# Value projection of the first layer in three column passes over four PSUM banks, with the gate columns in the first pass

## The chip, the cores and the metric

The kernel runs on one core of one Trainium2 chip. The metric is the device time of one launch in microseconds (us). The engines of the core work side by side: TensorE (PE, with its weight loads as PEld) does matmuls into PSUM, VectorE (DVE) and ScalarE (ACT) do elementwise work, GpSimd (POOL) does memsets here, and SyncE (SP) issues most of the loads and stores. PSUM has eight banks of 512 float32 columns in each of 128 partitions. This kernel hands them out as two `ps` tiles of one bank, two `pc` tiles of one bank and two `pm` tiles of two banks.

## The reference

The model has 1024 tokens of width 1024 and two layers: an mLSTM mixer with an MLP, then latent attention with an MLP. The change is in the mixer of the first layer. Of the reference, what it computes there:

```python
def mlstm_mixer(h, w_in, gate_b, head_g, w_out):
    proj = h @ w_in                      # (S, 3088)
    q, k, v, ig, fg, og = jnp.split(proj, splits, axis=-1)   # 512, 512, 1024, 8, 8, 1024
    ...
    i_pre = (ig + gate_b[0]).transpose(0, 2, 1)
    f_pre = (fg + gate_b[1]).transpose(0, 2, 1)
    hh = mlstm_chunkwise(heads(q, A_QK_DIM), heads(k, A_QK_DIM), heads(v, A_V_DIM), i_pre, f_pre)
    hh = rmsnorm(hh.transpose(0, 2, 1, 3), head_g).reshape(B_, S, A_V_W)
    return (hh * jax.nn.sigmoid(og)) @ w_out
```

There are eight heads. The values `v` are columns 1024 to 2047 of `w_in`, 128 for each head; the two gates are the 16 columns behind them, 2048 to 2063, one input gate and one forget gate for each head. `mlstm_chunkwise` goes over chunks of 128 tokens: inside a chunk it weighs scores of q and k by decays that come from the gates (running sums and running maxima along the tokens) and multiplies them with the values; between chunks it carries a state.

## The kernel before, in words

**Precision.** Every large product is made of three: an operand is split into a high part (`hi`, rounded to float32r) and the rest (`lo`), and `mm3` (L230 to L234) adds lo x hi, hi x lo and hi x hi in PSUM. So each matmul of a projection stands three times, on L232, L233 and L234.

**Weights.** `wload` (L204 to L224) loads a block of a weight matrix into one of four `raw` buffers of 128 x 1024 (L132), then `wsplit` casts it to its high part on ScalarE (L189) and subtracts that on VectorE to get the low part (L190). High and low parts take two of eight `ws` buffers, so four blocks can be ready ahead. `wload` runs at high priority. The `raw` buffers are taken in turn, in the order of the program, and they are shared with the background work below.

**Order.** The program is written out by generators that are woven into each other; then a scheduler orders the instructions of each engine by a simulated timeline, and may draw an instruction forward when its data and buffers are there. Buffers of a kind are always given out in the order of the program. `with_bg(g, bgs, n)` (L1880) runs n background steps for each step of g; `weave(main, fill, per)` (L71) and `weave_n` (L60) run `per` steps of a filling generator for each step of the main one; `weave` runs the rest of the filling one behind it, `weave_n` doesn't.

**Background.** `bgs` computes the modulation vectors of later stages. A chunk (`ada_chunk`, L348) loads four blocks of 512 KB into `raw` (L353), adds each, multiplied by the condition, into the one `tma` buffer on VectorE (L358 for the first row block, L360 for the other seven), makes two empty steps, and then turns the result with four transposes into a `pc` tile (`ada_turn`, L340) and reduces it on VectorE (L342, L343). That is seven steps, four of them with a load. The next chunk needs `tma` again.

**Halves.** The tokens are worked on in two halves of 512 (four tiles of 128). The normalised input of a half lies transposed, `h.hi[k]` and `h.lo[k]` for k of 0 to 7 (128 features x 512 tokens).

- `gates_in` (L626) of a half loads the 16 gate columns, spreads them over a zeroed 128 x 128 block for each k (the high parts at columns 0 to 7 and 32 to 39, the low parts at 64 to 71 and 96 to 103), and runs 16 matmuls of 512 columns into a `ps` tile (L642, L643): all of h goes through the array twice for 16 columns.
- `gates0` (L702) is a serial chain on VectorE and ScalarE over tiles of 8 x 512: the sums of the gates and biases (L707 to L711), log-sigmoid, running sums (L724), running maxima (L730), exponentials, the rows of `RM` (L744 to L751); then 12 small transposes (L756) and the copy of `gc` (L758).
- `qk_pairs` (half 0) and `qk_in` (L648, half 1) make queries and keys. In half 1 each of eight blocks is 24 matmuls of 512 columns into a `ps` tile, copied out on ScalarE (L198, L202).
- `v_in` (L657) makes the values with the tokens as rows: for each of four column blocks of 256 it loads two weight blocks (four k each); for each of four token tiles 24 matmuls of 256 columns go into one `ps` tile, which is copied to the value buffers on VectorE (L685) for odd tiles and on ScalarE (L687) for even ones. It makes 16 steps.
- `intra0` (L761) makes, for each of four pairs of heads, two decays (a matmul of a mask, L772, and one of `RM`, L775, into a `pc` tile, then four exponentials on ScalarE, L779, which need `gc`), eight score blocks into one `pm` tile (L787), their product on VectorE (L792), and a scaling of the queries (L795 to L797). It makes five steps for a pair.
- `chunks0` (L814) then goes over the chunks with `pm` tiles for the numerators (L831, L836); beside it run the output gates `og0` (L690, in `ps`) and, in half 0, the norm of the other half, `norm0`.

In half 0 `gates_in` comes first, with one background step for each of its three steps; then the activations of half 1 are loaded (`load_x1`), and then `v_in`, with one background step for each of its steps, runs woven with `intra0` at 1.5. In half 1 `gates_in` comes first too; then queries and keys (each step doubled by `twice`) and values form one main generator of 32 steps. Its first six steps run alone, with `split_o` of half 0 behind the fourth, and the rest runs with 1.7 background steps and 0.8 steps of `intra0` for each.

## Time and profile before

| | |
|---|---|
| median of 3 runs | 2370.01 us (2367.67 to 2371.02) |
| the profiled execution | 2373.3 us |
| its span, first to last instruction | 2371.2 us |
| granted TensorE clock | 0.996 |
| TensorE busy | 2334.8 us |
| VectorE, ScalarE busy | 1605.2 us, 1099.8 us |

A row of the timeline reads: start in us from the beginning of the span, duration in us, engine, line of the code, operation, output<-inputs, shape, number of merged instructions, and in brackets the idle time before it with what ended it. A row of the groups reads: line, engine, operation, names and shapes, count, then busy us, mean ns of one, and the idle us of the engine just before them. The shape of a matmul gives the stationary block and the moving one: 128x512 is 512 moving columns. Matmuls overlap, so a duration is longer than the distance from one start to the next. SPq is the queue of SyncE, where loads are issued.

### The profile page before, as it was taken

How to read it: one execution, taken by the hardware profiler on the slowest of the kernel's cores; microseconds unless marked ns; L12 is line 12 of the kernel's file. 1: busy time of each engine (PE TensorE's matmuls, PEld its weight loads, DVE VectorE, ACT ScalarE, POOL GpSimd, SP SyncE). 2: the span in 40 equal slices, each digit the busy share in tenths (PEclk: the TensorE clock that was granted, in tenths of full speed). 3: DMA queues.
4: the chain of work that ended last, by engine and by line, in shares of the span. 5: the costliest groups of instructions: out<-in, count | busy, mean ns of one | idle time of the engine just before them, and what ended most of it. 6: DMA issues, size and time to landing. Idle time of an engine off the chain costs nothing.

```text
span 2371.2 us, 32533 instructions
## 1 busy us (share of the span) xinstructions
PE 2334.8 (98%) x12197; PEld 1967.3 (83%) x12197; DVE 1605.2 (68%) x2657; ACT 1099.8 (46%) x1826; POOL 147.6 (6%) x345
## 2 busy tenths in 40 slices
PE   7999999999999999999999999999999999999998
PEld 5888888788888888888888888888888888989997
DVE  6667866868666677877774967766566478457556
ACT  4355334655333464434444544434434445655543
POOL 1000000000001210111110110001001000000000
PEclk9999999999999999999999999999999999999999
DMA  9453564544656966667754675885544552657552
GB/s 312 143 145 89 181 184 137 170 130 150 187 178 166 313 184 197 185 200 205 227 157 117 196 208 176 269 272 167 173 129 132 147 169 86 189 175 218 165 183 89
DMA packets 408350, 420.77 MB, mean 177 GB/s; under 512 B 27427, under 2 KB 310112, under 8 KB 404608
## 3 DMA queue, kind: packets, MB, share of 16 engines
q1 hardware_dynamic: 402272, 385.02, 51.9%
q0 software_dynamic: 5920, 33.66, 6.5%
q8 instruction: 96, 1.57, 0.3%
q14 instruction: 62, 0.51, 0.1%
HBM read 359.37 MB, written 92.80 MB: 191 GB/s over the span
## 4 chain that ended last, share of the span: by engine, by line
PE 90%; DVE 4%; DMA 3%; ACT 2%; issue 1%; SPq 0%; DVEq 0%; ACTq 0%
PE ps L232 16%; PE ps L233 15%; PE ps L234 15%; PE pm L232 10%; PE pm L233 10%; PE pm L234 10%; PE pc L234 2%; PE pc L232 2%; PE pc L233 2%; DMA raw<-in_mlp_w_dram 1%; PE pc L1637 1%; DMA raw<-in_a_w_in_dram 1%; DVE wl L190 1%; PE pm L836 1%; PE pm L1523 1%
## 5 line engine op out<-in xcount | busy, mean ns | idle before, releaser
L190 DVE TENSOR_TENSOR wl<-raw,wh 128x1024 fp32r<-128x1024 f32 (+2 forms) x382 | 458.5, 1203 | 385.8 <-ACT wh L189 281.4
L189 ACT CAST wh<-raw 128x1024 fp32r<-128x1024 f32 (+2 forms) x382 | 394.0, 1035 | 657.9 <-PE ps L232 241.8
L232 PE MATMUL ps<-k,wl 128*128 128x512 f32 (+1 forms) x1464 | 560.3, 383 | 2.6 <-ACT k L695 1.4
L234 PE MATMUL ps<-k,wh 128*128 128x512 f32 (+1 forms) x1464 | 551.6, 377 | 0.0
L233 PE MATMUL ps<-k,wh 128*128 128x512 f32 (+1 forms) x1464 | 550.7, 376 | 0.0
L232 PEld LDWEIGHTS ps<-k,wl 128*128 128x128 f32 x1464 | 275.7, 188 | 56.5 <-issue 3.6
L234 PEld LDWEIGHTS ps<-k,wh 128*128 128x128 f32 x1464 | 275.5, 188 | 51.7 <-issue 0.7
L233 PEld LDWEIGHTS ps<-k,wh 128*128 128x128 f32 x1464 | 275.9, 188 | 50.0 <-issue 1.9
L198 DVE TENSOR_TENSOR k<-k,pm 128x512 f32<-128x512 f32 (+1 forms) x254 | 211.2, 860 | 87.2 <-PE pm L234 86.1
L232 PE MATMUL pm<-hd,wl 128*128 128x512 f32 x512 | 201.1, 393 | 0.5 <-ACT hd L472 0.5
L233 PE MATMUL pm<-hd,wh 128*128 128x512 f32 x512 | 199.5, 390 | 0.2 <-DVE hd L473 0.2
L234 PE MATMUL pm<-hd,wh 128*128 128x512 f32 x512 | 199.4, 390 | 0.0
L232 PE MATMUL pm<-wh,hd 128*128 128x512 f32 x488 | 192.2, 394 | 3.9 <-ACT raw L1529 3.7
L233 PE MATMUL pm<-wl,hd 128*128 128x512 f32 x488 | 190.5, 390 | 0.0
L234 PE MATMUL pm<-wh,hd 128*128 128x512 f32 x488 | 190.3, 390 | 0.0
L360 DVE SCALAR_TENSOR_TENSOR tma<-raw,cond,tma 128x512 f32<-128x512 f32 x168 | 125.7, 748 | 20.0 <-DMA raw<-in_kv_ada_w_dram 13.8
L1529 ACT ACTIVATE raw<-pm,sm 128x128 f32<-128x128 f32 (+3 forms) x64 | 47.4, 741 | 155.1 <-DVE sm L1528 118.2
L473 DVE TENSOR_TENSOR hd<-tmp,hd 128x512 fp32r<-128x512 f32 x128 | 88.0, 689 | 40.4 <-ACT hd L472 39.8
L232 PEld LDWEIGHTS pm<-hd,wl 128*128 128x128 f32 x512 | 96.2, 188 | 20.9 <-ACT hd L472 0.9
L233 PEld LDWEIGHTS pm<-hd,wh 128*128 128x128 f32 x512 | 96.2, 188 | 20.5 <-DVE hd L473 0.5
L234 PEld LDWEIGHTS pm<-hd,wh 128*128 128x128 f32 x512 | 96.2, 188 | 20.2
L985 POOL COPY sm<-sm 128x1 f32<-128x1 f32 x128 | 51.9, 412 | 967.2 <-DVE sm L984 930.3
(385 smaller groups left out, 4064.1 us busy)
## 6 DMA issues: line engine op xcount, KB each, us to landing
raw<-in_mlp_w_dram SPq DMA_DIRECT2D x240, 512.0 KB, 4.3
raw<-in_ada_w_dram SPq DMA_DIRECT2D x80, 512.0 KB, 4.3
raw<-in_a_w_in_dram SPq DMA_DIRECT2D x48, 512.0 KB, 4.8
sums<-in_mlp_w_dram POOLq DMA_DIRECT2D x96, 256.0 KB, 4.8
raw<-sums SPq DMA_DIRECT2D x64, 256.0 KB, 3.7
xs<-k SPq DMA_DIRECT2D x40, 256.0 KB, 3.6
raw<-in_kv_ada_w_dram SPq DMA_DIRECT2D x16, 512.0 KB, 3.9
raw<-in_a_w_out_dram SPq DMA_DIRECT2D x16, 512.0 KB, 5.0
```

The lines of the kernel that those rows point to most:

```text
L189: nc.scalar.copy(hi[:, :n], r[:, :n])
L190: i = nc.vector.tensor_sub(lo[:, :n], r[:, :n], hi[:, :n].bitcast(F32))
L198: return f(*a, **k)
L232: nc.tensor.matmul(o, ll, rh, start=start, stop=False, **m)
L233: nc.tensor.matmul(o, lh, rl, start=False, stop=False, **m)
L234: pe_last[0] = nc.tensor.matmul(o, lh, rh, start=False, stop=stop, **m)
L360: nc.vector.scalar_tensor_tensor(acc, r[:, kk], cond[:, k : k + 1], acc, ALU.mult, ALU.add)
L473: nc.vector.tensor_sub(lo, u, hi.bitcast(F32))
L836: nc.tensor.matmul(nv[:, r, i], hf.PT[p_][:, r, cs], v[2 * p_ + r], start=g == 0, stop=True,)
L985: now = nc.gpsimd.tensor_copy(seen, flag)
L1523: nc.tensor.matmul(o[:, :w], qh, kh, start=False, stop=True)
L1529: nc.scalar.activation(pr[:, :n], f, AF.Exp, bias=m, scale=SCALE, accum_out=l)
```

## The change

Values and gates of a half are made together. `v_in` goes over three column passes. The first holds heads 6 and 7 and the 16 gate columns (256 + 16 = 272 columns, which lie side by side in `w_in`), the second heads 0 to 2 and the third heads 3 to 5 (384 columns each). A pass holds the sums of all four token tiles in both `pm` tiles, one bank for each token tile, and goes over k in groups: three k to a weight block in the first pass (three blocks), two in the others (four blocks each), so eleven weight blocks instead of eight. After every second token tile of a weight block there is a step: 22 steps. In the last k group of a pass the finished banks are copied out, the even tile on ScalarE and the odd one on VectorE.

The gate columns now come out with the tokens as rows. VectorE copies them into a zeroed `tmp` tile, and `gates_in` turns them with four transposes into a `pc` tile. They hold the full sum, so `gates0` drops its additions of a low part (two copies go, two fused operations become plain ones). The scores of `intra0` move from a `pm` tile to the two `ps` tiles.

The order changes with it. In half 0 the first pass (six steps) runs before `load_x1`, then the gate chain and `intra0` are woven into the other passes at 1.5; background steps run at 0.73 for each of the 22 steps. In half 1 the first pass runs before the queries and keys, with `split_o` before its last step; queries, keys and the other passes then run with 1.5 background steps for each, and the gates and `intra0` at 0.8.

The diff (in `v_in` cut to its core):

```diff
@@ gates_in
-        h = hf.h
-        wg = raw(F32R).rearrange("p (a b) -> p a b", b=P)
-        nc.gpsimd.memset(wg.bitcast(F32), 0.0)
...
-        gp = ps()
-        for k in range(KD):
-            nc.tensor.matmul(gp, wg[:, k], h.lo[k], start=k == 0, stop=False)
-            nc.tensor.matmul(gp, wg[:, k], h.hi[k], start=False, stop=k == KD - 1)
+        gp = pc()
+        for t in range(4):
+            nc.tensor.transpose(gp[0:64, ts(t, P)], hf.graw[:, t], ident)
         hf.gp = gp
@@ v_in
-        for j in range(4):
-            w0 = wload([(0, 0, wcols(w_in, 1024 + j * 256, 256, 0, 4))], 256)
-            w1 = wload([(0, 0, wcols(w_in, 1024 + j * 256, 256, 4, 4))], 256)
...
+        hf.graw = tmp()[:, :256].rearrange("p (t c) -> p t c", c=64)
+        nc.gpsimd.memset(hf.graw, 0.0)
+        for h0, nh, kg in ((6, 2, 3), (0, 3, 2), (3, 3, 2)):
+            n = nh * P + (16 if h0 == 6 else 0)
+            b = [pm(), pm()]
+            for k0 in range(0, KD, kg):
+                nk = min(kg, KD - k0)
+                w = wload([(0, 0, wcols(w_in, 1024 + h0 * P, n, k0, nk))], n)
+                for t in range(4):
+                    for k in range(nk):
+                        kk = k0 + k
+                        mm3(
+                            b[t // 2][:, t % 2, :n], h.hi[kk][:, ts(t, P)], h.lo[kk][:, ts(t, P)],
+                            w[0][:, k], w[1][:, k], kk == 0, kk == KD - 1,
+                        )
+                    if t % 2 and k0 + nk == KD:
+                        b2 = b[t // 2]
+                        if h0 == 6:
+                            nc.vector.tensor_copy(
+                                hf.graw.rearrange("p t (g c) -> p t g c", c=32)[:, t - 1 : t + 1, :, 0:8],
+                                b2[:, :, 256:272].rearrange("p t (g c) -> p t g c", c=8),
+                            )
+                        for e in range(2):
...
+                            copy = nc.vector.tensor_copy if e else nc.scalar.copy
...
                     if t % 2:
...
+                        yield
@@ gates0
-        nc.vector.tensor_copy(t1, gp[64:72])
-        nc.vector.scalar_tensor_tensor(t1, gp[0:8], col(GB, 1)[0:8], t1, ALU.add, ALU.add)
-        nc.vector.tensor_copy(t2, gp[96:104])
+        nc.vector.tensor_scalar(t1, gp[0:8], col(GB, 1)[0:8], None, ALU.add)
         nc.vector.tensor_copy(t3, gp[32:40])
-        nc.vector.scalar_tensor_tensor(t2, t3, col(GB + 1, 1)[0:8], t2, ALU.add, ALU.add)
+        nc.vector.tensor_scalar(t2, t3, col(GB + 1, 1)[0:8], None, ALU.add)
@@ intra0
-            st = pm()
+            st = [ps(), ps()]
...
-                        st[:, r, ts(j, P)], kp[ts(r, 64), ts(j, P)], qp[ts(r, 64), ts(j, P)],
+                        st[r][:, ts(j, P)], kp[ts(r, 64), ts(j, P)], qp[ts(r, 64), ts(j, P)],
...
-                nc.vector.tensor_mul(PT[:, r], st[:, r], E[r])
+                nc.vector.tensor_mul(PT[:, r], st[r], E[r])
@@ the order
-    drain(with_bg(gates_in(hfs[0]), bgs, 1))
+    main = with_bg(v_in(hfs[0]), bgs, 0.73)
+    for _ in range(6):
+        next(main)
     x1 = load_x1()
-    drain(weave(with_bg(v_in(hfs[0]), bgs, 1), intra0(hfs[0]), 1.5))
+    drain(weave(main, chain(gates_in(hfs[0]), intra0(hfs[0])), 1.5))
...
-    drain(gates_in(hfs[1]))
-    main = chain(twice(qk_in(hfs[1])), v_in(hfs[1]))
-    for _ in range(4):
-        next(main)
-    drain(split_o(hfs[0]))
-    for _ in range(2):
-        next(main)
-    drain(weave_n(with_bg(main, bgs, 1.7), intra0(hfs[1]), 0.8))
+    v1 = v_in(hfs[1])
+    for n in range(6):
+        next(v1)
+        if n == 4:
+            drain(split_o(hfs[0]))
+    main = chain(twice(qk_in(hfs[1])), v1)
+    drain(weave_n(with_bg(main, bgs, 1.5), chain(gates_in(hfs[1]), intra0(hfs[1])), 0.8))
```

More of the change, by code (lines that the diff above doesn't have):

```diff
@@ new lines, in v_in @@
+        nc.gpsimd.memset(hf.graw, 0.0)
[20 more added lines that the diff above has]
+                        for e in range(2):
+                            i = b2[:, e, : nh * P].rearrange("p (a b) -> p a b", b=P)
+                            v = hf.v[t - 1 + e]
+                            copy = nc.vector.tensor_copy if e else nc.scalar.copy
+                            if h0 == 6:
+                                for o in range(2):
+                                    copy(v[6 + o][:, 0:128], i[:, o])
+                            else:
+                                copy(v[8][:, h0 : h0 + 3, 0:128], i)
@@ L684, in v_in @@
                     if t % 2:
-                        nc.vector.tensor_copy(o, a)
-                    else:
-                        nc.scalar.copy(o, a)
-                yield
+                        yield
     def og0(hf, alloc):
```

24 lines of the change are left out of this document (removed).

## Prediction

> **What bounds the kernel now.** I read the page first, then the two stages that the change touches (busy time by stretch, and who waited for whom on TensorE), then TensorE's rows in order of time, and last the rows of the queues that feed it. The page:
>
> ```profile
> PE 2334.8 (98%) x12197; PEld 1967.3 (83%) x12197; DVE 1605.2 (68%) x2657; ACT 1099.8 (46%) x1826; POOL 147.6 (6%) x345
> ...
> PEclk9999999999999999999999999999999999999999
> ...
> PE 90%; DVE 4%; DMA 3%; ACT 2%; issue 1%; SPq 0%; DVEq 0%; ACTq 0%
> ```
>
> TensorE is busy 98% of the span at the full granted clock, and 90% of the chain that ends last is TensorE. So a TensorE microsecond that goes is a microsecond gained, if nothing else comes late in its place. The stretch of the values in each half (half 0, then half 1 from its first query projection), then the waits of TensorE over both:
>
> ```profile
> 84.70:146.50 61.80, 60.45 (x487) 56.38 (x487) 45.34 (x87) 26.92 (x72) 0.00 (x0) 1.00 0.46 132
> 222.70:325.50 102.80, 101.61 (x672) 89.32 (x671) 84.19 (x141) 35.86 (x70) 0.00 (x0) 1.00 0.60 184
> ```
>
> ```profile
> PE ps L232 <- DVE wl L190: 1.0, 1, 1.0
> PE ps L232 <- DVE k L685: 0.8, 1, 0.8
> PE pc L772 <- ACT tmc L779: 0.5, 1, 0.5
> ```
>
> The columns of the first two rows are the stretch, its length, the busy time of PE, PEld, DVE, ACT and POOL, the clock, the DMA share and GB/s. TensorE idles about 1.3 us in each. There is hardly a wait to win: the gain has to come out of TensorE's own work.
>
> **The change part by part. The price of a matmul.** Matmuls overlap, so their durations say nothing; I take the distance between starts. First and last of a run of 48 matmuls of 512 columns (the last row is the start of the next run), then of 24 of 256 columns:
>
> ```profile
> 52.29 0.39 PE L232 MATMUL pm<-k,wl 128*128 128x512 f32 x1
> ...
> 63.17 0.39 PE L232 MATMUL ps<-k,wl 128*128 128x512 f32 x1
> ...
> 290.38 0.28 PE L232 MATMUL ps<-wh,k 128*128 128x256 f32 x1
> ...
> 293.26 0.39 PE L772 MATMUL pc<-identb,maskA 128*128 128x512 bf16 x1
> ```
>
> 10.88 us / 48 = 226.7 ns and 2.88 us / 24 = 120.0 ns. A straight line through both is 13.3 ns plus 0.417 ns a column, so 272 columns cost 126.7 ns and 384 cost 173.4 ns. Both lie between two measured widths, so I keep no spread for them.
>
> *Value matmuls.* Before: 4 column blocks x 4 token tiles x 8 k x 3 products = 384 a half, 384 x 0.1200 = 46.08 us. After: 96 in each pass, 96 x (0.1267 + 2 x 0.1734) = 45.46 us. Saved 0.62 us a half, 1.25 us in both: 96 fixed parts go, 16 columns are added. The Trainium skill, "TensorE: Matmul & The Clock Gate", section "Back-to-back issue gap", gives N/2.4 + 2.5 ns, with a fixed part of 2.5 ns instead of 13.3 ns. By it the passes would grow from 41.9 to 42.3 us a half, and the direct sum below would be a gain of 5.2 us instead of 7.9. The trace disagrees (226.7 ns against 215.8 at 512 columns), and the trace decides.
>
> *Gate matmuls go*, 16 of 512 columns a half, first and end rows of each run (in half 1 a run of 9 and one of 7):
>
> ```profile
> 80.13 0.39 PE L642 MATMUL ps<-k,raw 128*128 128x512 f32 x1
> ...
> 83.85 0.93 PE L787 MATMUL pm<-k,k 64*128 64x128 f32 x10
> ...
> 218.45 0.48 PE L642 MATMUL ps<-k,raw 128*128 128x512 f32 x1
> ...
> 220.62 0.60 PE L894 MATMUL pc<-ident,tmc 128*128 128x128 f32 x4
> 220.97 0.48 PE L643 MATMUL ps<-k,raw 128*128 128x512 f32 x1
> ...
> 222.67 0.39 PE L232 MATMUL ps<-k,wl 128*128 128x512 f32 x1
> ```
>
> 3.72 + 2.17 + 1.70 = 7.59 us. *Four transposes a half come*; the nearest row is a turn of four 128x128 blocks:
>
> ```profile
> 276.73 0.60 PE L340 MATMUL pc<-ident,tma 128*128 128x128 f32 x4
> 277.08 0.36 PE L232 MATMUL ps<-wh,k 128*128 128x256 f32 x1
> ```
>
> 0.35 us, and the matmul after it starts about 0.1 us late: 0.45 us a half, 0.9 in both. **Direct sum: -1.25 - 7.59 + 0.9 = -7.94 us.**
>
> *Work beside TensorE.* The preparation of weights and the copies out of PSUM:
>
> ```profile
> L190 DVE TENSOR_TENSOR wl<-raw,wh 128x1024 fp32r<-128x1024 f32 x366 | 446.5, 1223 | 382.3 <-ACT wh L189 278.4 <-PE pm L233 47.4 <-ACT tmp L1060 17.2
> L190 DVE TENSOR_TENSOR wl<-raw,wh 128x768 fp32r<-128x768 f32 x8 | 7.6, 954 | 2.2 <-ACT wh L189 2.2
> L685 DVE COPY v<-ps 128x128 f32<-128x128 f32 x4 | 1.1, 282 | 0.0
> L758 DVE COPY gc<-pc 128x96 f32<-128x96 f32 x2 | 0.5, 258 | 2.6 <-PE pc L756 2.6
> L707 DVE COPY tmc<-ps 8x512 f32<-8x512 f32 x2 | 1.4, 684 | 1.8 <-PE ps L643 1.8
> ```
>
> Eleven loads of 816, 544 or 768 columns instead of eight of 1024: VectorE 2 x 1.00 + 0.72 + 8 x 0.95 = 10.3 us (the two odd sizes by the line through the two rows) instead of 9.8 a half. Two copies like L707 (0.68 us each) go from the gate chain. VectorE idles 27% and 18% of the two stretches and ScalarE more, so I cost all of that at nothing; with the cover gone it would be under 1 us a half. The deleted gate DMA, its casts and POOL's memset of a whole weight buffer cover nothing that anyone waits for; two small POOL memsets take their place.
>
> *PSUM at the end of a pass.* The accumulators now fill both pm buffers, and a pass can't start on the first of them until the one before is copied out. Cover: the last k group of the other two tiles, 12 x 0.1267 = 1.52 us after pass 1 and 12 x 0.1734 = 2.08 us after pass 2. Need on VectorE after pass 1: about 0.26 + 2 x 0.28 = 0.82 us. An undisturbed copy is hidden; one queued behind a weight split (1.22 us) is late by 0.5 us. The transposes wait for the copy of the gate columns, and pass 2 is queued behind them on TensorE: the same wait, not a second one. A late copy has a row in the kernel before (the 0.8 us wait on L685 above, with the old cover of 2.9 us), so 0 to 4 us in all; I take 0.5.
>
> *Scores in ps.* In half 1 two of the four score blocks fall among the query and key projections, which live in the same two ps buffers. A projection then waits for the score matmuls and the multiply (L787, L792):
>
> ```profile
> L787 PE MATMUL pm<-k,k 64*128 64x128 f32 x128 | 12.0, 294 | 0.0
> L792 DVE TENSOR_TENSOR hd<-pm,tmc 128x512 f32<-128x512 f32 x16 | 10.9, 686 | 3.6 <-ACT tmc L779 3.6
> ```
>
> The score matmuls themselves are the same (12.0 us / 8 = 1.5 us a block). What is new is up to 0.7 us of multiply plus the copy of the last projection before each, 0 to 2 us each; I take 1.0 in all, 0 to 4.
>
> **The late gates of half 0** are the part that can eat the gain. Before, the gate chain on VectorE starts at 83.96 and ends with the copy of gc; only then may the exponentials run, and only then the turn of a background chunk (L340), which takes its pc buffer behind the gates' in program order:
>
> ```profile
> 83.96 0.69 DVE L707 COPY tmc<-ps 8x512 f32<-8x512 f32 x1 [1.77 <-PE ps L643]
> 103.72 0.26 DVE L758 COPY gc<-pc 128x96 f32<-128x96 f32 x1 [2.10 <-PE pc L756]
> 108.35 0.60 PE L340 MATMUL pc<-ident,tma 128*128 128x128 f32 x4
> 110.10 0.75 DVE L360 SCALAR_TENSOR_TENSOR tma<-raw,cond,tma 128x512 f32<-128x512 f32 x1
> 79.50 4.86 SPq L353 DMA_DIRECT2D raw<-in_ada_w_dram  x3
> 110.88 2.72 SPq L211 DMA_DIRECT2D raw<-in_a_w_in_dram  x2
> 115.68 1.23 DVE L190 TENSOR_TENSOR wl<-raw,wh 128x1024 fp32r<-128x1024 f32 x1
> ```
>
> Between 83.99, the last of the three issues of the 79.50 row, and 110.88 no load is issued at all: the four raw buffers are filled with background chunks, whose first operations (L358, L360) wait for the one tma buffer, which the turn at 108.35 frees. Eight weight buffers, four pairs, carry TensorE through this: 4 x 48 matmuls of 120 ns = 23 us, and the score blocks of all four head pairs that had been drawn ahead. So it ran dry only then, for 0.5 us (the third wait above).
>
> After the change I count the same ring. The raw buffers are taken in the order of the program: weights 1 to 3 of pass 1 and 4 to 7 of pass 2 take turns with background loads 1 to 5; weight 8, the first of pass 3, takes the buffer of background load 5, the first of the second chunk. Its operations need tma, so again the turn, so again the end of the gate chain. Now that chain starts later: pass 1 starts at 80.1, lasts 12.2 us and one score block of 1.5 us (only one, as both ps buffers stay taken until its multiply), then come copies and transposes, so about 94.9. It takes 20.0 us (83.96 to 103.98) less 1.4 us, so gc is there at 113.5. From the turn to the end of the weight's low half it was 108.35 to 116.91, 8.6 us; so weight 8 is ready at about 121. Pass 2 ends at 93.8 + 0.4 + 16.6 = 110.8, a little later with the small transposes of the gate chain. For these 10 us TensorE has only those and the scores and decays of the first pairs, in half 0 in all:
>
> ```profile
> L787 PE MATMUL pm<-k,k 64*128 64x128 f32 x62 | 6.1, 297 | 0.0
> L775 PE MATMUL pc<-RM,e 128*128 128x512 f32 x8 | 4.5, 560 | 0.0
> L795 PE MATMUL pc<-RM,selW 128*128 128x512 f32 x4 | 1.8, 448 | 0.0
> ```
>
> 12.4 us / 4 = 3.1 us a pair, two pairs if nothing holds them up, one if their exponentials do; so 3 to 6 us idle if nothing else is drawn forward, against 0.5 us in the row of before. Between these ends I take 3.0: the ring and the order are read from rows, but where the scheduler puts the turn among the gates I can't see. The old waits of this stretch (0.8 + 0.5 us, together the 1.35 us that TensorE idles in it) are gone with the buffers and the moment that made them. Where this stall goes, pass 3 is late next, then the chunks (L831, L836), which need all four pairs.
>
> The rest is re-paced, not changed: 16 instead of 19 background steps by the end of half 0, 48 instead of 44 in half 1, cost nothing as long as the ring follows.
>
> **Sum:** -7.94 - 1.35 + 3.0 + 0.5 + 1.0 = -4.8 us. The profiled execution took 2373.3 us (span 2371.2, 2.1 us around it), so 2368.5; it lies 3.3 us above the median of the runs, 2370.0, from which I forecast **2365.2 us**. A measurement of this kernel can tell about 0.2% from no change, 4.7 us: the forecast lies just at that edge.
>
> **The rivals.** *All is hidden.* The turn or weight 8 comes early enough, so that the late gates cost 0 to 0.5 us and the copies nothing: -7.94 - 1.35 + 1.0 = -8.3 us, 2361.7. For it: TensorE is nearly gapless in both stretches, and the scheduler drew score blocks (the 83.85 row) 20 us ahead of the exponentials. Against it: the 27 us without a load.
>
> *The gain is eaten in half 0.* The whole 6 us are paid, and 1.5 us at the passes and at the scores: -9.3 + 7.5 = -1.8 us, 2368.2: no change that can be told. For it: the dependence of the turn on the gates, which held the second chunk back for 39 us (its first buffer was loaded at 70.70 and used at 109.59). Against it: a scheduler that draws work forward.
>
> ```profile
> 70.70 0.37 SPq L353 DMA_DIRECT2D raw<-in_ada_w_dram  x1
> 109.59 0.48 DVE L358 TENSOR_SCALAR tma<-raw,cond 128x512 f32<-128x512 f32 x1
> ```
>
> *Slower: weights bound half 1.* In passes 2 and 3 a weight load feeds 24 x 173.4 ns = 4.2 us of TensorE instead of 48 x 120 ns = 5.8 us, and at 1.5 background steps a yield, four of seven steps with a load, 1.7 background loads come with it: 2.7 raw buffers per 4.2 us and the small work between, some 5.5 us. A buffer is held for a landing and about 2.3 us of work, some 7 us, so four give about 3.1 per 5.5 us: an eighth to spare.
>
> ```profile
> raw<-in_a_w_in_dram SPq DMA_DIRECT2D x28, 512.0 KB, 4.8
> ```
>
> If the ring falls behind by the 1.0 us of the old L190 wait at each of 16 loads, 16 us come on top: -9.3 + 1.5 + 16 = +8 us, 2378. It decides from the point at which more than half of the loads are late by 1 us. Against it: DMA is busy 0.60 of this stretch, and one such wait in the whole of it.
>
> *The passes don't do what they say*, their matmuls keeping 120 ns per 256 columns or worse, would show in the first row of the new widths; with 226.7 and 120.0 ns on one line I give it no chance of its own, nor the smaller fixed part that the page states.
>
> **How the numbers follow.** Forecast 0.44; all hidden 0.24; eaten 0.20; slower by the ring 0.12. The forecast's own spread (3.0 between 0.5 and 6, the two small terms between 0 and 4) is about 2361 to 2370, and lies half on each side of the edge. Faster by over 0.2%: 0.24 + half of 0.44 = 0.46, and a little of the eaten case, 0.48. Slower by over 0.2%: the ring and the far ends of two small terms, 0.14. The rest, 0.38, is within 0.2%. The range leaves out the far half of the ring's case and the best tenth of the hidden one: 2358 to 2373.
>
> **What would show it.** Right: 384 columns at 173 ns and 272 at 127 ns from start to start; no matmul on L642 or L643; four transposes in 0.35 us; a gate chain in half 0 that starts near 95 and a gap of TensorE between 111 and 122 that ends on a weight of a_w_in; no load issued by SP for a long while before. Wrong: no gap there (the hidden case), gaps before matmuls on pm that end on the copies out of pm or, in half 1, on L190 again and again (the ring). If TensorE's busy time falls by 7.9 us and the span doesn't, the working of the passes held and the waits ate it; if the busy time doesn't fall, the price of a matmul was wrong.

## The result and the profile after

The changed kernel takes 2394.89 us (median of 4 runs, 2391.2 to 2400.02), the kernel before in the same comparison 2370.32 us (4 runs). The ratio is 1.0103, with a 95% interval of 1.009 to 1.0116: slower by 24.6 us, outside the forecast range on the side to which 0.14 had been given. The profiled execution took 2394.44 us (span 2392.7), 21.1 us more than the one of before. The page of the changed kernel, busy time, granted clock and chain:

```profile
PE 2339.5 (98%) x11981; PEld 1966.6 (82%) x11981; DVE 1600.7 (67%) x2655; ACT 1099.7 (46%) x1824; POOL 145.8 (6%) x345
...
PEclk9999899999999999999999999999999999999999
...
PE 84%; DMA 6%; DVE 6%; ACT 2%; issue 1%; SPq 0%; DVEq 0%; ACTq 0%
```

The share of TensorE still reads 98%, and it executes 216 matmuls fewer. What has moved is the chain (TensorE 90% to 84%, DMA 3% to 6%) and one slice of the clock, the fifth, 239 to 299 us. To find where the time went, I take four instructions that both kernels have, in order of time; of the kernel before:

```profile
208.05 0.68 DVE L864 TENSOR_REDUCE sm<-tmc 128x4 f32<-128x512 f32 x1
...
381.24 0.16 DVE L432 SCALAR_TENSOR_TENSOR sm<-sm,sm 128x4 f32<-128x4 f32 x1
...
840.74 1.22 DVE L198 TENSOR_TENSOR k<-k,pm 128x1024 f32<-128x1024 f32 x1 [1.68 <-PE pm L234]
...
2361.14 0.16 DVE L430 TENSOR_TENSOR sm<-sm 128x1 f32<-128x1 f32 x1 [0.80 <-ACT sm L429]
```

And the same four in the changed kernel (L859 is the old L864):

```profile
207.04 0.68 DVE L859 TENSOR_REDUCE sm<-tmc 128x4 f32<-128x512 f32 x1
...
395.46 0.16 DVE L432 SCALAR_TENSOR_TENSOR sm<-sm,sm 128x4 f32<-128x4 f32 x1
...
864.27 1.22 DVE L198 TENSOR_TENSOR k<-k,pm 128x1024 f32<-128x1024 f32 x1 [1.69 <-PE pm L234]
...
2382.38 0.16 DVE L430 TENSOR_TENSOR sm<-sm 128x1 f32<-128x1 f32 x1 [0.81 <-ACT sm L429]
```

The difference is -1.0 us after half 0, +14.2 after half 1, +23.5 in the first layer's MLP, +21.2 at the end. So half 0 won a microsecond, half 1 lost 15, the way through the MLP lost 9 more, and 2 came back later. The busy time by stretch, from the first gate or value matmul of each half; before, then after:

```profile
80.10:147.10 67.00, 65.65 (x519) 60.53 (x518) 47.51 (x90) 28.84 (x75) 0.00 (x0) 1.00 0.46 135
218.45:329.15 110.70, 109.50 (x721) 96.11 (x719) 90.70 (x148) 41.56 (x82) 0.00 (x0) 1.00 0.59 181
```

```profile
79.40:146.00 66.60, 64.22 (x406) 57.93 (x405) 46.02 (x85) 29.92 (x73) 0.00 (x0) 1.00 0.46 132
217.30:344.10 126.80, 115.88 (x611) 98.85 (x609) 89.17 (x150) 40.41 (x80) 0.00 (x0) 0.93 0.51 157
```

The second row of each ends with the last value matmul of half 1; I call this stretch the stage of half 1. It grew from 110.7 to 126.8 us: TensorE idles 10.9 us in it instead of 1.2, and is "busy" 6.4 us longer on 110 matmuls fewer, mostly because the granted clock fell to 0.93 of full speed (the score matmuls take longer too, as shown below). Who was late, in TensorE's waits of the changed kernel between 217 and 345 us:

```profile
PE pm L232 <- ACT wh L189: 3.1, 2, 1.8
PE pc L751 <- ACT tmc L736: 2.4, 1, 2.4
PE pc L751 <- ACT tmc L738: 1.3, 1, 1.3
PE pc L770 <- DVE RM L746: 1.1, 1, 1.1
PE pc L767 <- DVE sm L342: 0.8, 1, 0.8
PE ps L232 <- DVE wl L190: 0.7, 1, 0.7
```

Weights (L189, L190) and the gate chain (L736 to L746). TensorE's rows of the changed kernel show the first hole:

```profile
246.44 0.39 PE L234 MATMUL ps<-k,wh 128*128 128x512 f32 x1
246.76 0.22 PE L751 MATMUL pc<-ident,tmc 8*128 8x8 f32 x1
246.91 0.66 PE L340 MATMUL pc<-ident,tma 128*128 128x128 f32 x4
248.35 0.38 PE L767 MATMUL pc<-identb,maskA 128*128 128x512 bf16 x1 [0.78 <-DVE sm L342]
251.11 0.27 PE L751 MATMUL pc<-ident,tmc 8*128 8x8 f32 x1 [2.39 <-ACT tmc L736]
252.71 1.23 PE L751 MATMUL pc<-ident,tmc 8*128 8x8 f32 x10 [1.33 <-ACT tmc L738]
...
257.65 0.80 PE L232 MATMUL ps<-k,wl 128*128 128x512 f32 x1 [0.66 <-DVE wl L190]
258.25 0.63 PE L233 MATMUL ps<-k,wh 128*128 128x512 f32 x1
258.67 0.63 PE L234 MATMUL ps<-k,wh 128*128 128x512 f32 x1
```

The last projection for which there is a weight ends at 246.7; the next starts at 257.65. Between them TensorE follows the gate chain step by step. It takes those steps because nothing else is there, and the weight is not there because of SP, whose rows say when loads were issued; the changed kernel, then the kernel before:

```profile
219.01 12.48 SPq L353 DMA_DIRECT2D raw<-in_ada_w_dram  x3
251.42 4.74 SPq L211 DMA_DIRECT2D raw<-in_a_w_in_dram  x2
```

```profile
220.17 10.47 SPq L353 DMA_DIRECT2D raw<-in_ada_w_dram  x3
249.31 0.37 SPq L211 DMA_DIRECT2D raw<-in_a_w_in_dram  x1
```

Both kernels then issue no load for 19 to 20 us: the four raw buffers hold a background chunk that waits for tma, and so for the turn (L340). In the kernel before the turn came at 245.3, only 1.6 us earlier, and the weight 2.1 us earlier. But there TensorE had 16 gate matmuls and five blocks of 24 projection matmuls, to 252.9, and then score matmuls until the weight was ready at 255.75. In the changed kernel the first pass of the values has gone ahead of the projections and used up three weights, the gate matmuls are gone, and three blocks of projections are through at 246.7.

After the gap the two 512-column matmuls at 258.25 and 258.67 start 0.42 us apart, not 0.227. The granted clock in the changed kernel's stretches around it:

```profile
247.00:257.60 10.60, 4.25 (x19) 2.43 (x19) 9.54 (x20) 4.56 (x11) 0.00 (x0) 0.62 0.21 60
257.60:266.00 8.40, 8.35 (x25) 6.44 (x25) 4.14 (x5) 1.85 (x5) 0.00 (x0) 0.67 0.95 286
```

8.40 x (1 - 0.67) = 2.8 us are lost behind the gap to the clock alone.

About half of the 9 us lost on the way through the MLP is a wait of TensorE on a background turn, here between 400 and 880 us; before, then after:

```profile
PE pc L340 <- DVE tma L360: 1.1, 1, 1.1
```

```profile
PE pc L340 <- DVE tma L360: 5.8, 2, 3.6
```

That is 4.7 us more. One wait for a copy grew by 0.8 us (1.4 to 2.2), and the granted clock is 0.97 between 420 and 480 us and between 600 and 660 us, where the kernel before has 1.00: by estimate 60 x 0.03 = 1.8 us in each.

### The profile page after: what moved, and what is told of

It reads as the page before. It is cut to its first block, busy times and chain, and to the rows that moved or that the text cites. A ratio compares the mean times of both kernels' runs of the same rounds, so it can differ in the third digit from the quotient of the medians.

```text
span 2392.7 us, 32128 instructions
## 1 busy us (share of the span) xinstructions
PE 2339.5 (98%) x11981; PEld 1966.6 (82%) x11981; DVE 1600.7 (67%) x2655; ACT 1099.7 (46%) x1824; POOL 145.8 (6%) x345
## 4 chain that ended last, share of the span: by engine, by line
PE 84%; DMA 6%; DVE 6%; ACT 2%; issue 1%; SPq 0%; DVEq 0%; ACTq 0%
PE ps L232 14%; PE ps L233 13%; PE ps L234 13%; PE pm L232 10%; PE pm L233 9%; PE pm L234 9%; DMA raw<-in_mlp_w_dram 4%; PE pc L234 2%; PE pc L232 2%; PE pc L233 2%; DVE wl L190 1%; DMA raw<-in_a_w_in_dram 1%; PE pc L1632 1%; ACT wh L189 1%; DVE tma L360 1%
## 5 line engine op out<-in xcount | busy, mean ns | idle before, releaser
L190 DVE TENSOR_TENSOR wl<-raw,wh 128x1024 fp32r<-128x1024 f32 (+2 forms) x388 | 459.8, 1187 | 411.3 <-ACT wh L189 314.6
L189 ACT CAST wh<-raw 128x1024 fp32r<-128x1024 f32 (+2 forms) x388 | 395.4, 1022 | 696.9 <-PE ps L232 237.6
L360 DVE SCALAR_TENSOR_TENSOR tma<-raw,cond,tma 128x512 f32<-128x512 f32 x168 | 125.6, 748 | 29.3 <-DMA raw<-in_kv_ada_w_dram 16.1
```

Of the source, the lines that this page charges most:

```text
L189: nc.scalar.copy(hi[:, :n], r[:, :n])
L190: i = nc.vector.tensor_sub(lo[:, :n], r[:, :n], hi[:, :n].bitcast(F32))
L360: nc.vector.scalar_tensor_tensor(acc, r[:, kk], cond[:, k : k + 1], acc, ALU.mult, ALU.add)
```

## The experiments

Three theories stood at the start. *Ring*: in half 1 the weights stand behind background loads in the four raw buffers, and the small blocks and the later gates leave TensorE nothing to do meanwhile. *Scores*: the two heads of a score block lost an overlap when they got separate tiles. *Steps*: the number of background steps (16 and 48 instead of 19 and 44) shifts what comes later. "Stage" is the stretch of half 1 defined above: 110.7 us before, 126.8 after.

**The scores, in the changed kernel.** The rows of score blocks, before and after:

```profile
253.02 1.39 PE L787 MATMUL pm<-k,k 64*128 64x128 f32 x20
254.33 0.39 PE L772 MATMUL pc<-identb,maskA 128*128 128x512 bf16 x1
```

```profile
268.19 1.16 PE L782 MATMUL ps<-k,k 64*128 64x128 f32 x8
269.28 0.39 PE L767 MATMUL pc<-identb,maskA 128*128 128x512 bf16 x1
```

20 matmuls in 1.31 us, against 8 in 1.09 us: 65 ns each against 136. e1 issues the two heads in turn again.

```
+            prev = None
             for j in range(4):
-                for r in range(2):
-                    nc.tensor.matmul(
+                for r in (1, 0):
+                    with tc.issue_after(prev.ins) if prev else nullcontext():
+                        prev = nc.tensor.matmul(
```

> The changed kernel with one edit: the eight score matmuls of a pair of heads are issued strictly in turn, one of one head, one of the other, as they stood in the kernel before. Theory 'lost overlap': in the kernel before the score matmuls of the two heads start 7 ns apart in twos (64 of them take 5.05 us of the stretch of half 1), in the changed one they stand four and four, 112 ns apart (8.01 us), 2.6 and 3.0 us in the two halves; in turn again, their rows start in twos and the time falls by 4 to 6 us. Rival 'late background alone': the scores overlap again in the rows, but the time stays within 1.5 us, as TensorE waits for weights anyway. Rival 'two ps buffers': the starts stay 112 ns apart, as the two tiles come free one after the other.

It took 2399.21 us, ratio 1.0116 (1.0099 to 1.0133). The score matmuls got their overlap back (13.4 us busy for 128, against 17.5), but each block now waits for both ps buffers at once, 3.7 us in one place, and the stage came out at 131.5 us. The time is 27.5 us over the kernel before of the same comparison, not told from the 24.6 of the changed kernel, so none of the three expectations came as written. Getting the overlap back in this way gains nothing. e4 takes the overlap away from the kernel before:

```
-            for j in range(4):
-                for r in range(2):
+            prev = None
+            for r in range(2):
+                for j in range(4):
+                    with tc.issue_after(prev.ins) if prev else nullcontext():
```

> The kernel before with one edit: the eight score matmuls of a pair of heads are issued four of one head, then four of the other, in the same pm tile; nothing else. Theory 'lost overlap': the scores take 2.5 to 3 us more in each half, and the time rises by 4 to 6 us. Rival: TensorE has slack there or the order costs nothing by itself, and the time stays within 1.5 us.

2374.31 us against 2371.69, ratio 1.0009 (0.9999 to 1.0018): about 2.6 us, between the two expectations and not told from nothing. The score matmuls of e4, against 12.0 us in the kernel before and 17.5 in the changed one:

```profile
L789 PE MATMUL pm<-k,k 64*128 64x128 f32 x128 | 15.3, 290 | 0.0
```

If that carries over to the changed kernel, the scores cost 2 to 3 us of the 24.6; no run shows it there by itself.

**The background in half 1, late.** e2 lets the first 8 steps of the main work of half 1 pass without background:

```
-    drain(weave_n(with_bg(main, bgs, 1.5), chain(gates_in(hfs[1]), intra0(hfs[1])), 0.8))
+    main = chain(itertools.islice(main, 8), with_bg(main, bgs, 1.5))
+    drain(weave_n(main, chain(gates_in(hfs[1]), intra0(hfs[1])), 0.8))
```

> The changed kernel with one edit: in half 1 the first eight steps of queries and keys run without background steps, the rest at 1.5 as before (36 steps instead of 48; the other twelve come later). Theory 'ring behind the gates': the turn of a background chunk waits for its pc buffer behind the late gates, its tma and the raw buffers stay taken, and the fifth weight block of half 1 is loaded only at 251; without background there the gap of TensorE between 247 and 258 and the lower clock after it go, and the stretch of half 1 is 8 to 10 us shorter. Rival 'gates at the head of the queue': TensorE waits for the gate chain itself (transposes of the gates queued ahead of the projections), so the gap stays at 6 us or more. Rival 'small weight blocks': the gap is from the eleven smaller loads, and nothing changes. The whole time is not told apart by this, as twelve steps move to the stages behind: down by 5 to 10 us if those hide them, unchanged if not.

2388.36 us, ratio 1.0065 (1.0049 to 1.0081). The hole at 247 is gone (PE busy 10.52 of the 12 us from 247 to 259) and the stage takes 115.1 us. But 8 yields without background are 12 steps that are still owed: TensorE waits for turns (the old L340) 2.6 us before 480 and 6.2 us behind it.

**One step less.** e3 has 47 steps in half 1, 63 in all as before.

```
-    drain(weave_n(with_bg(main, bgs, 1.5), ...
+    drain(weave_n(with_bg(main, bgs, 1.47), ...
```

> The changed kernel with one edit: 1.47 instead of 1.5 background steps in half 1, so that 63 steps have run at its end (16 and 47), as in the kernel before (19 and 44), and not 64. Theory 'phase of the background': the 5.8 us that TensorE waits in the first MLP for VectorE before a turn (two waits, 3.6 and 2.2 us, against one of 1.1 us before) come from the background being one step further at the start of that stage; with 63 steps they fall to about 1.1 us, and the time falls by 5 to 7 us. Rival 'late MLP': the waits come from the shift of that whole stage by 17 us against nothing in particular, or from the loads, and stay; the time is unchanged within 2 us.

2390.1 us, ratio 1.0074 (1.0057 to 1.0091): 18.4 us over the kernel before of the same comparison instead of 24.6, so 6.2 us less, as the steps theory said. The wait on L340 in the MLP fell from 5.8 to 2.5 us, not all the way to 1.1. In the profiled execution half 1 took 130.1 us, with waits for weights of 7.8 and 3.5 us. That execution was the longest of the four (2393.97 us, the others 2387.0 to 2391.15), so it is not shown that half 1 is slower with 47 steps than with 48. What the trace does show is that one step less moves the waits to other weights: the largest is now on L190, before projections (7.8 us in three waits, against one of 0.7).

**No background in half 1.** e5 takes it out of the weave; its steps run behind the stage, so nothing is left out.

```
-    drain(weave_n(with_bg(main, bgs, 1.5), chain(gates_in(hfs[1]), intra0(hfs[1])), 0.8))
+    drain(weave_n(main, chain(gates_in(hfs[1]), intra0(hfs[1])), 0.8))
```

> The changed kernel with one edit: no background steps at all beside the projections of half 1 (48 steps fewer there; they come at once behind that stage). Theory 'ring behind the gates': without background the four raw buffers carry weights alone, no wait for weights (L189, L190) is left in half 1 and its stretch is 10 us or more shorter than in the changed kernel, at about the length it had before (it lost 15.6 us to the kernel before). Rival 'small weight blocks': eleven smaller blocks don't keep up even alone, waits for weights of 1 us and more stay in passes 2 and 3. Rival 'gates at the head of the queue': the gap near 247 to 258 stays at 5 us or more, as it is the gate chain that TensorE waits for. The whole time is no measure, as the 48 steps fall on the stages behind.

e12 is the control, the kernel before with the same taken out (`with_bg(main, bgs, 1.7)` becomes `main`).

> Control to the run of the changed kernel without background steps in half 1, here the kernel before without them (all 44 run behind the stage). It prices the direct saving of half 1 with the ring out of the way. The changed kernel took 107.5 us there from the first value matmul to the last. If the direct sum of the prediction holds for one half (0.62 of value matmuls, 3.87 of gate matmuls, less 0.45 of transposes: 4.0 us), and the scores cost 1.5 to 3 us of it, this takes 109 to 110 us from the first gate matmul to the last value matmul. If it takes 107 or less, nothing is left of the saving even without the ring. The time as a whole is expected at 2380 to 2400, from steps left over at the end of the stage.

As wholes they take 2410.93 us (ratio 1.0174, 1.0157 to 1.0191) and 2411.27 (one run), with the dumped steps behind the stage. The stage is what they are for; the changed kernel without background, then the kernel before without it:

```profile
217.20:324.70 107.50, 107.12 (x587) 93.19 (x585) 54.41 (x91) 38.48 (x79) 0.00 (x0) 0.97 0.27 79
```

```profile
217.30:325.20 107.90, 107.69 (x695) 94.02 (x693) 51.88 (x85) 38.31 (x79) 0.00 (x0) 1.00 0.23 69
```

Two things follow. Without background the small blocks keep TensorE fed (0.4 us idle, and no wait for a weight is left): 384 columns per load alone don't starve it. And the saving of half 1, 4.0 us by the prediction's direct sum, is only 0.4 us even here, between the two marks of e12's expectation. The clock column says why, in the changed kernel without background:

```profile
252.60:256.20 3.60, 3.55 (x29) 3.03 (x29) 3.48 (x6) 1.71 (x3) 0.00 (x0) 0.99 0.00 0
256.20:262.90 6.70, 6.37 (x14) 4.24 (x14) 2.44 (x9) 2.21 (x8) 0.00 (x0) 0.50 0.20 59
```

6.7 us at half clock cost 3.35 us, most of the 3.6 that are missing. They follow 3.6 us in which TensorE has score matmuls of 64 rows, 8x8 transposes of the gate chain and a single matmul of 512 columns; in the kernel before such work (253.02 to 255.75, 2.7 us) lies between projections, and the clock stays at 1.00.

**The gates drawn ahead.** e6 gives the gates of half 1 priority in front of the weave.

```
+    with tc.high_priority(PRIO):
+        drain(gates_in(hfs[1]))
-    drain(weave_n(with_bg(main, bgs, 1.5), chain(gates_in(hfs[1]), intra0(hfs[1])), 0.8))
+    drain(weave_n(with_bg(main, bgs, 1.5), intra0(hfs[1]), 0.69))
```

> The changed kernel with one edit: in half 1 the gate chain is written ahead of the queries and keys and at high priority, and the pairs of heads follow at 0.69 steps. In the changed kernel the gate columns are copied at 231.0 to 231.3, but their transposes stand behind 29 matmuls of a projection and start at 236.5, so the chain starts 5.8 us late. Theory 'late gates': the chain starts within 1 us of the copy, all that hangs on it (the turn, tma, the fifth weight block, loaded at 251) comes 5 us earlier, and the time falls by 5 to 8 us. Rival 'ring alone': the weights wait for the background's own loads and VectorE's work on them, and the time stays within 2 us. Rival 'mostly passes 2 and 3': only the gap near 247 to 258 shrinks, and the stalls before weights behind 318 grow by as much.

2403.44 us, ratio 1.0142 (1.0125 to 1.0159): worse. The chain started no earlier (L704 at 237.9 against 237.1), the turn came later, behind the exponentials, and the weight made TensorE wait 8.7 us in one piece. None of the three expectations came. The moment of the gates can't be set by this means, and it was not shown what early gates would bring.

**Private buffers.** In e8 the raw buffers of half 1 are parted: two for weights, two for the background.

```
+    def share(on):
+        mine[0] = None
+        if on:
+            four = [raw() for _ in range(4)]
+            mine[0] = four[:2], four[2:]
...
-            r = buf()[:, :1024]...
+            r = (raw_bg if buf is raw else buf)()[:, :1024]...
...
+    share(True)
     v1 = v_in(hfs[1])
...
+    share(False)
     drain(bg0)
```

> The changed kernel; in the first layer's second half the four raw buffers are parted: two for the weights of the projections and values, two for the background chunks, so that a weight no longer takes the buffer of a background load that waits for the turn behind the gates. Ring theory: the idle 6 us at 247 to 258 and the waits of L232 on L189 in passes 2 and 3 go, the stage from the first value matmul of half 1 to the last comes down from 126.8 us to 107 to 114, and the time from 2394.9 to 2379 to 2384; the loss in the first layer's MLP, which hangs on the number of background steps, stays. Rival (SP issues in order, and a background load that waits for its own buffer holds the weights behind it; or two buffers are too few for a 512 KB load each 4.2 us): the stage stays above 120 us and the time above 2390.

2385.87 us, ratio 1.0058 (1.0043 to 1.0073): 13.8 us over the kernel before of the same comparison instead of 24.6, so 11 us are back; the time came out 2 us above the range that the ring theory gave. The stage takes 113.5 us, as it said, and the two waits of TensorE in it no longer name a weight (in this kernel's numbering L784 is the old L770, L760 the old L746, L801 the old L787):

```profile
PE pc L784 <- DVE RM L760: 1.5, 1, 1.5
PE ps L246 <- DVE hd L801: 1.5, 1, 1.5
```

SP's row shows why (L225 is the old L211):

```profile
219.80 37.45 SPq L225 DMA_DIRECT2D raw<-in_a_w_in_dram  x8
```

Eight weight loads and no background load are issued between 219.8 and 257.3, where the changed kernel issued no load at all for 20 us, although the turn of the waiting chunk comes later here (252.0 against 246.9). So what TensorE lacked in the changed kernel was not an earlier turn: its weights shared their buffers with loads that waited for the turn. This is the ring theory shown: the same blocks, the same gates, the same 48 steps in the program (21 background loads issued in the shorter stage instead of 24), and 13.3 us less in the stage. What that stretch still has over the 107.5 us of e5 is a wait for the gates' chain (the first row above), one for the multiply of a score block (the second), and the turns; the clock is 0.97 in both.

The control is e9, the kernel before with the same parting.

> Control: the kernel before with the same parting of the raw buffers in the second half. Ring theory: there the shared ring cost hardly anything (1.2 us of gaps in the stage), so the time is within 3 us of 2370. If the parting itself helps by more than 3 us, or costs more than 3 us, what e8 shows is not the ring alone.

2378.86 us, ratio 1.0032 (1.002 to 1.0044): 6.7 us worse, so this expectation failed, and by its own words the time of e8 is not the ring alone. Its stage is fine (110.0 us), but with two buffers the background falls behind, and right after the stage TensorE waits 5.4 us for a turn. So parting has a price of its own behind the stage. What it costs in e8 was not shown (there is no such wait behind e8's stage), so the 11 us that came back are what the shared ring cost, less that price; the stage is the cleaner measure. e10 adds the step count of e3 to e8 (1.47 for 1.5):

> As e8, with 47 background steps in the second half instead of 48 (63 in all, as before). Both causes treated: ring theory and phase theory together expect e8's time less about 4 us (the 6.7 us of the MLP back to about 2), 2375 to 2380, still not under 2370, as the lost overlap of the scores (2 to 3 us) and the turns of pass ends stay. Rival: the two are not independent, and the time is e8's or worse.

2380.32 us, ratio 1.0032 (1.0018 to 1.0046). That is 0.3 us above the expected range. The steps theory holds again: the wait on the old L340 behind the stage falls from 5.0 us in e8 to 1.8. With both causes treated it is 8.2 us over the kernel before of its comparison (2372.12): 16.4 of the 24.6 us are back. What is left arises in half 1: in its trace the lag on the kernel before is 7.6 us where that half ends and 7.5 at the end.

**One half alone.** e7 has half 0 as changed, with 19 background steps there (0.87 for 0.73), and half 1 as before, with 44.

> Half 0 as in the changed kernel, half 1 as in the kernel before (its gates, values, scores and order), with 19 background steps in half 0 (0.87 a step) and 44 in half 1, so that all behind stands as before. Theory 'the loss is half 1 and the phase of the background': half 0 alone gains about 1 us by the trace, so the time is that of the kernel before within 3 us, most likely 0 to 2 us lower. Rival 'each half pays': half 0 costs as well, by new waits that the trace of the changed kernel hides behind a faster start, and the time is 4 us or more above the kernel before.

2380.03 us, ratio 1.0042 (1.0027 to 1.0057), 10.2 us over the kernel before, as the rival said. In the trace half 0 ends 5.1 us late, with a wait of 2.8 us for the copies of the values (L683) and 1.7 us for an exponential; half 1 adds nothing, and the way through the MLP adds 3.0. The profiled execution was the fastest of the four, so the trace shows about half of the 10.2 us. e11 has half 0 with the change's own 16 steps, and 47 in half 1 of before (1.81 for 1.7).

> Half 0 as in the changed kernel, with its 16 background steps; half 1 as in the kernel before, with 47 instead of 44 (63 in all, as before). Ring theory: the passes pay where the background is thin, so half 0 ends about 1.2 us earlier; half 1 of before, with its blocks of 5.4 to 5.8 us a load, has room for three more steps at 0 to 3 us; the number of steps in all is that of before, so the MLP keeps its phase. 2368 to 2373, the same as before within what can be told. Rival (the passes themselves are worse wherever they stand, as the run with 19 steps in half 0 suggests): half 0 loses some 5 us here too, 2375 to 2379.

2377.74 us, ratio 1.0024 (1.0015 to 1.0033), inside the rival's range, but not for its reason. Half 0 cost next to nothing (0.7 us), but three steps more in the old half 1 cost 5 us, more than the 0 to 3 of the ring theory: a wait of 1.0 us for a weight (L189), one of 3.4, and the low clock behind that:

```profile
PE ps L232 <- DVE wl L190: 3.4, 1, 3.4
```

So the kernel before stands close to the edge itself.

**How many steps.** e13 is the changed kernel with 44 steps in half 1 (1.375 for 1.5), e14 the same with parted buffers.

> The changed kernel with 44 background steps in half 1, as many as the kernel before has there (60 in all). The kernel before with 47 steps in half 1 lost 5 us to a weight that came late. If the denser background is the larger part of the loss of half 1, its stage comes down from 126.8 us to 115 to 119 and the time, apart from the MLP's phase, by 8 to 12 us: 2382 to 2388. If the smaller blocks and the later gates are the larger part, the stage stays at 122 to 127 us and the time at 2390 or above.

> The same with the raw buffers of half 1 parted, two for weights and two for the background: no background load stands before a weight, and fewer of them come. If what is left of the loss is the ring, this is at most 112 us from the first value matmul to the last, and 2378 to 2384 in all; if what is left is the low clock and the gates behind the projections, the stage stays at 113 to 115 us as it was with 48 steps.

2401.15 us (ratio 1.0126, 1.0109 to 1.0143) and 2390.26 (1.0078, 1.0063 to 1.0093). As wholes they are worse than with 48 steps, since the steps left over are paid later. The stage is 120.2 and 113.4 us, the first between its two expectations, the second in the range given for the case that the low clock and the gates are what is left; of e13:

```profile
217.20:337.45 120.25, 111.88 (x611) 97.12 (x610) 85.05 (x145) 39.05 (x79) 0.00 (x0) 0.94 0.49 150
```

Four steps fewer take 6.6 us off the stage as long as the ring is shared (126.8 to 120.2), and nothing once it is parted (113.5 and 113.4). So what the steps did to this stage they did through the ring. These are single traces, and with 47 steps the trace of e3 had 130.1 us, so the 6.6 is no price of a step.

## Why the prediction was wrong

*Prices of the matmuls: right.* 272 columns, two rows of the changed kernel 24 starts apart:

```profile
79.43 0.28 PE L232 MATMUL pm<-wh,k 128*128 128x272 f32 x1
...
82.45 0.29 PE L233 MATMUL pm<-wl,k 128*128 128x272 f32 x1
```

3.02 us / 24 = 125.8 ns (forecast 126.7); 384 columns, eight starts from 92.56 to 93.95:

```profile
92.56 0.33 PE L232 MATMUL pm<-wh,k 128*128 128x384 f32 x1
...
93.95 0.34 PE L234 MATMUL pm<-wh,k 128*128 128x384 f32 x1
```

1.39 us / 8 = 173.8 ns (173.4). The gate matmuls are gone, and four transposes cost 0.35 us (236.45 to 236.80).

*Half 0: near, for another reason.* Its terms make -2.1 us (half the direct sum, -1.35, 3.0, and half of the 0.5 for copies); it came out at -1.0. The gap between 111 and 122 did not come. (The working has a slip too: 113.5 + 8.6 is 122.1 for weight 8, not 121.) The scheduler had drawn forward the work of all pairs, and TensorE waited 0.4 us there; a wait of 1.6 us for a copy came with the chunks, which the prediction had named as late next. So the 3.0 us of the gap were 2.4 us of other waits (with 0.4 at L839), and the score blocks took longer, 8.9 us busy in this stretch against 6.1; that the sum comes out near is luck in part.

*"The score matmuls themselves are the same (12.0 us / 8 = 1.5 us a block)": wrong.* They take 17.5 us instead of 12.0, part of it at the low clock; e4 prices the lost overlap in the kernel before at 3.3 us of TensorE and about 2.6 us of time.

*The step that failed: "The rest is re-paced, not changed: 16 instead of 19 background steps by the end of half 0, 48 instead of 44 in half 1, cost nothing as long as the ring follows."* The ring did not follow, and a term that stood at nothing was the largest: parting the ring (e8) takes 13.3 us off the stage and 11 us off the time. I had counted the ring load by load for half 0, where the turn behind the late gates holds the second chunk, and did not make the same count for half 1, where the change does the same thing under worse conditions: there the first value pass moves ahead of the projections, so that the work which had covered 19 us without a load has been spent before that stretch begins. The count was to be had from the kernel before: the weight issued there at 249.31 is used at 255.75, with the last cover just gone.

*The rival "weights bound half 1" had the right place and half of the mechanism.* It put 1.0 us on each of 16 loads and held that 4 buffers have an eighth to spare. What came was a hole of 6 us behind the gates, waits of 1 to 2 us in passes 2 and 3, and the clock, which no term had: 126.8 - 110.7 = 16.1 us against the 16 of the rival. That agreement is chance: the 16.1 are what is left after the direct saving, the 16 were to come on top of it. Its mark for decision, L190 again and again, did not show as such: L189 twice and L190 twice, with the gate chain in front. It stood at 0.12 since one wait in the old trace was taken for slack; e11 shows that three more steps would have found its end.

*The direct sum was too large where the clock falls.* e5 and e12 leave 0.4 of 4.0 us in half 1; the clock had no term.

*Not foreseen: the MLP.* 64 steps in all instead of 63 put the turns of a later chunk where TensorE must wait for them, 5.8 us against 1.1; with 63 steps it is 2.5 (e3) and 1.8 (e10).

Of the 24.6 us, e10 gets 16.4 back. Of the 8 that remain in it, 2 to 3 may be the scores, if e4 carries over; how the rest divides between the gate chain, the clock, and the price of parting was not settled. No version tried beats the kernel before.

## What to carry to other kernels

When loads of two kinds take turns in one ring of buffers, count the ring in every stage that a change touches: what the oldest waiting load waits for, and how many microseconds of matmuls are still covered when it is let go. Moving work ahead of a stall uses up the cover that hid it, even when the sum of the work falls. A stage with hardly any waits may be at its edge rather than have room; one run with a few more loads tells.

## What the runs showed of the hardware

The clock halved behind light work, not only behind idle time: in e5 TensorE was busy 3.55 of 3.6 us with small matmuls before the 6.7 us at 0.50. The Trainium skill, "TensorE: Matmul & The Clock Gate", section "Part 1: The HAM clock gate", says that the clock is set by how busy the array has been and falls to half after an idle window of about 3.4 us. The half clock agrees (0.50; the matmuls at 258.25 and 258.67 of the changed kernel lie 0.42 us apart); that it also falls behind a stretch in which the profile shows TensorE busy is what this run adds. The stretch need not be light throughout. In e4 the clock halved in half 0 behind 3.41 us without a wait, filled with eight score matmuls (four of one head, then four of the other), eleven 8x8 transposes and six value matmuls; the kernel before has 1.00 in both of these stretches:

```profile
99.99:103.40 3.41, 3.41 (x29) 2.86 (x28) 1.08 (x3) 0.37 (x1) 0.00 (x0) 0.99 0.00 0
103.40:106.80 3.40, 3.40 (x16) 3.30 (x16) 0.87 (x2) 1.14 (x4) 0.00 (x0) 0.50 0.00 0
```

I have not varied the length or the mix of the light stretch, so its threshold stays open.

Score matmuls of 64 rows cost 65 ns each when the two heads alternate and 136 ns when four of one head follow each other: up to twice the price. In e4 nothing but their order differs, and it is enough for 15.3 us instead of 12.0, on average 120 ns against 94.
